# Seven row blocks of a hybrid decoder layer turned by transposing DMAs in place of TensorE, and the last value block of two FFN parts computed by feature

## The chip, the cores and the metric

The kernel runs on one core of a Trainium2 chip. The metric is the device time of one execution in microseconds (us), the median of several runs. TensorE (PE) multiplies, VectorE (DVE) and ScalarE (ACT) work beside it, GpSimd (POOL) here does little but issue DMAs that accumulate, and SyncE (SP) issues nearly all other DMAs.

## The reference

One decoder layer for 256 tokens of width 2048, all in float32. What matters here is its row of dense products:

```python
merged = (sigmoid(g_a) * (ret_out @ w_proj_ret) + sigmoid(g_b) * (rnn_out @ w_proj_rnn))
h = h + merged @ w_mix_out
hn = rmsnorm(h, norm_xa_w)
mem_n = rmsnorm(mem, norm_mem_w)
h = h + memory_cross_attention(hn, mem_n, xa_w_q, xa_w_k, xa_w_v, xa_w_o)
hn = rmsnorm(h, norm_ffn_w)
up = causal_dwconv(hn @ w_up, conv_w, conv_b)     # 2 x 5632 columns
gate, val = split(up, 2)
h = h + (silu(gate) * val) @ w_down
return rmsnorm(h, final_norm_w)
```

## The kernel before

**Precision and weights.** A float32 product is made of three products of parts: each operand is split into a high part `hi` and a rest `lo`, and hi·hi, hi·rest and rest·hi are summed. All weights lie in one array in the order of use and are streamed in pieces of 1 MB (`raw`, 128x2048, six buffers). `prefetch` keeps two pieces ahead: SP loads `raw` (L265), ACT casts `hi` (L286), DVE subtracts `lo` (L287), and PE reads both. There are three buffers of `hi` and of `lo`, so the cast of a piece waits until PE is through with the piece three before it. One piece is one *unit*; `later(n, fn)` lets `fn` be written into the program n+1 units on, and it is in this way that all other work is placed between the units.

**Products.** A product of 512 output columns is four units (four groups of four 128-row chunks of the 2048). `gemm_n` gives it by token (tokens on the partitions) into one accumulator: 16 matmuls with `hi` (L362, L363) and 8 with `lo` (L369) a unit. `gemm_t` gives it by feature (output columns on the partitions) into two accumulators: 16 matmuls of 512 and 16 of 256 columns a unit (L351). Accumulators come from a pool of three. Two neighbouring blocks of columns can be made as a pair (`pair_add`, `pair_out`) by seven products in place of eight: 11 units in the order q1 p0 q3 p1 q5 q2 q6 p2 q7 q4 p3, where a p unit has 24 matmuls and a q unit 12. For these, operands must exist as sums too: `ss` (four subtractions and additions on DVE, L501 to L504, then L506 and L507), and sums of weights are made in the `raw` buffers A, B and C: after q5's `lo`, DVE adds B to A (L294); when that is done, POOL issues a DMA that accumulates the weights of q7 onto B (L267); and a further addition on DVE (L292) makes the weights of q4. ACT casts the pieces in the order of the units, each `hi` behind the one before it on its queue.

**Turning.** A product contracts over features, so a row block (256 tokens by 512 columns) that came by token must be turned, each half of it (256 columns) giving one `s` (its hi and rest). Two ways exist. On PE: `transposed` makes four 128x128 transposes (L532) per half block into a buffer of PSUM, `sm`, of which there are two, and ACT and DVE read it (`split_pair`, L555 and L556; `split_cols` with the norm's weight, L578 and L579). By DMA: `row_planes` copies the block's words as two planes of 16 bits (ACT, L757, `rp`), `turn_planes` issues two transposing DMAs on SP (L1205, into `d`), and `join_planes` puts the words of each half together again (ACT, L763, two copies into `jp`). Of the row blocks before the FFN, twelve go by PE: the four of `merged` (`turn_merged`), the four of the residual stream after `w_mix_out` and the four after `xa_w_o` (`turn`, with `URGENT` priority for the scheduler). The blocks of the FFN's up product (`up`) go by DMA.

**The FFN** is cut into parts of 4, 4 and 3 blocks. In a part each block is a gate product and a value product, both turned by DMA, then the causal convolution (`conv`: ACT L1281, DVE L1283), then `hidden` (L1354 to L1356, and the split L555, L556), which gives two pairs of `hid`. After a part of four, two `pair_add` of `ffn_w_down` read all eight of `hid` (pairs 6 and 7 come of the part's last value block). They begin right behind the product of the last value block, whose joins are due 2 and 4 units on. In the part of three the last value block is already made by `gemm_t`, with `scaled` (ACT copies half the accumulator, L544; DVE adds the other half, L545, and scales, L676).

Of the kernel before, what the change touches and what calls it, by code (L numbers as in the profile page):

```python
# [12 lines left out]
U16 = mybir.dt.uint16  # L13
# [141 lines left out]
def hybrid_layer(  # L155
# [37 lines left out]
    def tmp(s="t"):  # L193
        return tp.tile([P, 2, S], F32, tag="tmp", name=nm(s))
# [109 lines left out]
    def later(n, fn):  # L304

        pending.append((step[0] + n + 1, fn))
# [460 lines left out]

    class KeptRows(list):
# [247 lines left out]
    def turn_merged(m, pr):  # L1016
        for t in transposed(m[:, :, pr * S : (pr + 1) * S]):
            if len(merged) < KC:
                c = tmp("mt")
                act.mul(c, t, 0.5)  # L1020
                merged.append(split_pair(c))
                merged_sums.append(sums(c))
            else:
                merged.append(split_pair(t, 0.5))
# [95 lines left out]
    rsms = []  # L1120
# [14 lines left out]
    h1s, h1s_sums = [], []  # L1135
    ss1 = residual("w_mix_out", merged, merged_sums, h1s, h1s_sums, p_xa, memory_steps)
    hkept = dp.tile([4, P, 2, BW], F32, name="hkept")
    for b in range(4):
        sp.dma_start(out=hkept[b], in_=hrow[b])

# [44 lines left out]
    def row_planes(o):  # L1185

        t = big([P, 2, 2, BW], U16, s="rp")
        planes(t, o)
        return t

# [9 lines left out]

    def turn_planes(rows):

        d = big([P, 2, KC, S], U16, s="d")
        for tt in range(2):
            sp.dma_start_transpose(  # L1205
                out=d.rearrange("p a c s -> p (a c) s")[:, :, tt * P : (tt + 1) * P],
                in_=rows[:, tt].rearrange("p a w -> p (a w)"),
            )
        return d
# [153 lines left out]
    for part, nb_ in enumerate(FF_PARTS):  # L1363
# [3 lines left out]
        for b in range(b0, b0 + nb_):  # L1367
# [10 lines left out]
            up(FF, b, None if last and not paired else (2, 4) if last else (1, 2), finish_up)  # L1378
# [54 lines left out]
```

## Time and profile before

| what | value |
|---|---|
| median of 3 runs | 1997.41 us (1996.22 to 1998.04) |
| the profiled execution | 1995.6 us, its span 1993.8 us |
| PE busy | 1968.6 us, 99% of the span |
| DVE, ACT, POOL busy | 79%, 64%, 2% |
| granted TensorE clock, mean | 0.995 |
| HBM | 220 GB/s over the span |

A row of a timeline reads: start, duration, engine, line, operation, output <- inputs, how many, and in brackets the idle time before it with what ended it. A row of a group reads: count, then busy us and mean ns of one, then the idle time before them. In a table of windows each engine has its busy time and, in brackets, its instructions; PEclk is the granted clock as a share of full speed. SPq and POOLq are the queues on which these engines issue.

### The profile page before, as it was taken

What the parts mean: (1) busy time and instruction counts of PE and PEld (TensorE: products, weight loads), DVE (VectorE), ACT (ScalarE), POOL (GpSimd) and SP (SyncE); (2) the same over time, 40 slices, a digit from 0 to 9 for tenths busy, and PEclk for the clock granted to TensorE, in tenths of its full rate; (3) what the DMA queues carried; (4) which work ended last, traced back from release to release, by engine and by line L of the source; (5) the groups of instructions that cost most, each with busy time, mean ns of one, the idle gap of its engine ahead of it and who ended that gap; (6) DMA issues with size and microseconds to landing.
All of it is one profiled execution on the core that took longest, in us unless ns stands there. A gap on an engine that the chain in (4) does not pass through costs nothing.

```text
span 1993.8 us, 23634 instructions
## 1 busy us (share of the span) xinstructions
PE 1968.6 (99%) x9304; PEld 1650.8 (83%) x9304; DVE 1566.4 (79%) x1546; ACT 1277.2 (64%) x1323; POOL 43.2 (2%) x52
## 2 busy tenths in 40 slices
PE   9999999999999999999999999999989999899998
PEld 7888888888888888888888888888878888788887
DVE  6978888889886886779988778677786777885775
ACT  6655656767677554567778756567744667546662
POOL 0000000000000000000000000000000000000000
PEclk9999999999999999999999999999999999899999
DMA  9675674655887865878998748766777677686671
GB/s 369 233 261 147 223 264 161 230 190 160 266 260 220 248 250 190 252 256 258 270 259 235 267 125 271 236 226 204 234 232 273 207 219 236 204 278 228 211 245 61
DMA packets 146463, 456.59 MB, mean 229 GB/s; under 512 B 77744, under 2 KB 82480, under 8 KB 98608
## 3 DMA queue, kind: packets, MB, share of 16 engines
q1 hardware_dynamic: 139072, 410.51, 58.7%
q0 software_dynamic: 5760, 41.95, 11.6%
q10 hardware_dynamic: 1520, 2.63, 0.4%
q8 instruction: 73, 1.20, 0.2%
q14 instruction: 38, 0.31, 0.0%
HBM read 420.96 MB, written 16.78 MB: 220 GB/s over the span
## 4 chain that ended last, share of the span: by engine, by line
PE 91%; DVE 4%; ACT 2%; DMA 1%; issue 1%; SPq 0%; POOLq 0%; ACTq 0%; DVEq 0%
PE acc L362 25%; PE acc L363 25%; PE acc L369 24%; PE acc L351 14%; PE sm L518 2%; DVE lo L287 1%; ACT hi L286 1%; DMA raw<-in_wall 1%; PE acc L518 1%; PE sm L948 1%; PE sm L532 1%; DVE raw L294 0%; DVE fv L1283 0%; DMA d<-rp 0%; DVE tb L722 0%
## 5 line engine op out<-in xcount | busy, mean ns | idle before, releaser
L287 DVE TENSOR_TENSOR lo<-raw,hi 128x2048 fp32r<-128x2048 f32 (+1 forms) x420 | 950.9, 2267 | 297.8 <-ACT hi L286 297.0
L286 ACT CAST hi<-raw 128x2048 fp32r<-128x2048 f32 (+1 forms) x418 | 793.2, 1901 | 522.7 <-PE acc L363 374.8
L362 PE MATMUL acc<-hi,s 128*128 128x512 f32 x2008 | 787.3, 392 | 12.4 <-ACT hi L286 12.3
L363 PE MATMUL acc<-hi,s 128*128 128x512 f32 x2008 | 784.3, 391 | 0.0
L369 PE MATMUL acc<-lo,s 128*128 128x512 f32 x2008 | 501.1, 389 | 0.0
L362 PEld LDWEIGHTS acc<-hi,s 128*128 128x128 f32 x2008 | 378.6, 189 | 91.5 <-ACT hi L286 13.2
L363 PEld LDWEIGHTS acc<-hi,s 128*128 128x128 f32 x2008 | 378.9, 189 | 78.5 <-DVE s L556 1.0
L369 PEld LDWEIGHTS acc<-lo,s 128*128 128x128 f32 x2008 | 377.1, 188 | 78.3
L351 PE MATMUL acc<-s,hi 128*128 128x512 f32 x832 | 200.4, 392 | 2.1 <-DVE hi L284 1.5
L351 PEld LDWEIGHTS acc<-s,hi 128*128 128x128 f32 x832 | 153.5, 188 | 32.8 <-issue 1.6
L362 PE MATMUL acc<-hi,ss 128*128 128x512 f32 x320 | 125.8, 393 | 0.8 <-ACT o L454 0.6
L363 PE MATMUL acc<-hi,ss 128*128 128x512 f32 x320 | 124.7, 390 | 0.0
L763 ACT COPY jp<-d 128x512 uint16<-128x512 uint16 x132 | 93.4, 771 | 29.4 <-DMA d<-rp 29.3
L351 PEld LDWEIGHTS acc<-s,lo 128*128 128x128 f32 x832 | 107.1, 191 | 4.9 <-DVE lo L287 1.3
L351 PE MATMUL acc<-s,lo 128*128 128x256 f32 x832 | 110.5, 284 | 0.5 <-DVE lo L287 0.5
L369 PE MATMUL acc<-lo,ss 128*128 128x512 f32 x320 | 85.6, 389 | 0.0
L362 PEld LDWEIGHTS acc<-hi,ss 128*128 128x128 f32 x320 | 60.1, 188 | 14.5 <-ACT o L454 1.4
L369 PEld LDWEIGHTS acc<-lo,ss 128*128 128x128 f32 x320 | 60.1, 188 | 12.6
L363 PEld LDWEIGHTS acc<-hi,ss 128*128 128x128 f32 x320 | 60.1, 188 | 12.2
L267 POOL DMA_DIRECT2D raw<-in_wall x40 | 35.2, 880 | 1550.7 <-DVE lo L287 887.5
L427 DVE TENSOR_TENSOR nat<-nat,acc 128x512 f32<-128x512 f32 (+1 forms) x49 | 44.0, 910 | 14.9 <-PE acc L369 14.9
L292 DVE TENSOR_TENSOR raw<-raw,raw 128x2048 f32<-128x2048 f32 x20 | 45.8, 2288 | 0.4
(235 smaller groups left out, 1251.7 us busy)
## 6 DMA issues: line engine op xcount, KB each, us to landing
raw<-in_wall SPq DMA_DIRECT2D x333, 1024.0 KB, 5.0
raw<-in_wall POOLq DMA_DIRECT2D x40, 1024.0 KB, 8.2
fkept<-nat SPq DMA_DIRECT2D x12, 512.0 KB, 7.7
nat<-fkept SPq DMA_DIRECT2D x12, 512.0 KB, 5.6
xt<-in_x_t SPq DMA_DIRECT2D x11, 256.0 KB, 7.8
raw<-in_wall SPq DMA_DIRECT2D x5, 512.0 KB, 7.9
nat<-in_x ACTq DMA_DIRECT2D x4, 512.0 KB, 10.1
ret<-hr SPq DMA_DIRECT2D x4, 512.0 KB, 4.6
```

The lines of the kernel that those rows point to most:

```text
L267: pool.dma_start(out=raw, in_=src, accum_op=ALU.add)
L286: act.copy(hi[:, a:b], raw[:, a:b])
L287: dve.tensor_tensor(out=lo[:, a:b], in0=raw[:, a:b], in1=hi[:, a:b].bitcast(F32), op=ALU.subtract)
L292: dve.tensor_tensor(out=to, in0=to, in1=by, op=ALU.add)
L351: pe.matmul(a, part, sx, start=k == 0 and t == 0, stop=k == nk - 1 and t == 0, skip_group_check=True)
L362: pe.matmul(o, h, hi, start=start and kk == 0, stop=False, skip_group_check=True)
L363: pe.matmul(o, l, hi, start=False, stop=False, skip_group_check=True)
L369: pe.matmul(o, h, lo, start=False, stop=stop and kk == KC - 1, skip_group_check=True)
L427: dve.tensor_tensor(out=o, in0=o, in1=i, op=op)
L518: ins = pe.matmul(o, a, b, start=start and i == 0, stop=stop and i == 2, skip_group_check=True)
L532: ins = pe.transpose(t[:, j, tt * P : (tt + 1) * P], rows[:, tt, k + j * P : k + (j + 1) * P], ident)
L763: ins = act.copy(words(t)[:, :, :, 1 - i], d[:, i, 2 * pr : 2 * pr + 2, :])
```

## The change

1. `merged` blocks 0, 1 and 2 are turned by `turn_merged_by_dma`, block 3 by PE as before. The joins are written 2 or 3 units on (1 or 2 for block 2). The factor 0.5 goes into `split_pair` and `sums`; the separate ACT multiplication falls away.
2. The residual's blocks 0 and 1, after `w_mix_out` and after `xa_w_o`, are turned by `turn_by_dma`, blocks 2 and 3 by PE as before. After `w_mix_out` the joins stand 1 and 2 units behind the transposing DMAs, after `xa_w_o` 3 and 4.
3. The stores of `h`'s blocks 0 and 1 to memory (`hkept`) are issued inside `turn_by_dma`; those of 2 and 3 stay behind `w_mix_out`.
4. The last value block of the two FFN parts of four is made by `gemm_t`, as the part of three has it; its convolution and `hidden` are due 1 and 3 units on.

```diff
+    def turn_merged_by_dma(m, n):
+        d = turn_planes(row_planes(m))
+
+        def join(pr):
+            t = join_planes(d, pr)
+            merged.append(split_pair(t, 0.5))
+            if len(merged) <= KC:
+                merged_sums.append(sums(t, 0.5))
+
+        for pr in range(2):
+            later(n + pr, lambda pr=pr: join(pr))
...
-        for pr in range(2):
-            later(pr, lambda m=m, pr=pr: turn_merged(m, pr))
+        if b < 3:
+            later(0, lambda m=m, n=2 if b < 2 else 1: turn_merged_by_dma(m, n))
+        else:
+            for pr in range(2):
+                later(pr, lambda m=m, pr=pr: turn_merged(m, pr))
...
-                for pr in range(2):
-                    later(i if bs[0] and len(bs) > 1 else 2 * i + pr, lambda b=b, pr=pr: turn(b, pr, out, osum, wcol))
+                if b < 2:
+                    n, m = ((0, 3), (4, 7))[i] if len(RESIDUAL[w]) == 2 else ((0, 1), (1, 2))[i]
+                    later(n, lambda b=b, m=m - n: turn_by_dma(b, m, out, osum, wcol))
+                else:
+                    for pr in range(2):
+                        later(i if len(bs) > 1 else pr, lambda b=b, pr=pr: turn(b, pr, out, osum, wcol))
...
+    def turn_by_dma(b, m, out, osum, wcol):
+        d = turn_planes(row_planes(hrow[b]))
+        if b < len(keep):
+            keep[b]()
+
+        def join(pr):
+            t = join_planes(d, pr)
+            i = 4 * b + 2 * pr
+            if osum is not None and len(out) < KC:
+                for j in range(2):
+                    act.activation(t[:, j, :], t[:, j, :], AF.Identity, scale=wcol(i + j))
+                out.append(split_pair(t))
+                osum.append(sums(t))
+            else:
+                out.append(split_cols(t, lambda j: wcol(i + j)))
+
+        for pr in range(2):
+            later(m + pr, lambda pr=pr: join(pr))
...
-            up(FF, b, None if last and not paired else (2, 4) if last else (1, 2), finish_up)
+            if last and paired:
+                for pr, a in enumerate(gemm_t("ffn_w_up", 0, h2s, NT, FF + b * BW)):
+                    later(1 + 2 * pr, lambda pr=pr, z=scaled(a, "uz"): finish_up(pr, z))
+            else:
+                up(FF, b, None if last else (1, 2), finish_up)
```

The order of instructions on each engine is set when the program is built, and the change moves it. Three places matter below; the numbers in the names tell buffers apart, and line numbers above 1000 differ between the two kernels.

**ACT at the end of the first `pair_add` of a part's down product.** Before, from the cast for p2 to that for q4: the casts are for p2, q7 and q4, `fv` is the convolution of pair 7, and `s_1672` is pair 7's split.

```order
L286 CAST hi_1674_11226<-raw_1673_11224 128x2048
L555 ACTIVATE s_1663_11157<-fo_1662_11153 128x2x256
L286 CAST hi_1676_11244<-raw_1652_11075 128x2048
L1281 ACTIVATE fv_1606_10757<-jp_1669_11206,pf_80 128x256 x2
L286 CAST hi_1678_11261<-raw_1640_10996 128x2048
L555 ACTIVATE s_1672_11221<-fo_1671_11217 128x2x256
```

And in the changed kernel, where `hi_1681`, `hi_1683` and `hi_1685` are the casts for p2, q7 and q4, and `s_1677` is pair 7's split:

```order
L555 ACTIVATE s_1669_11174<-fo_1668_11170 128x2x256
L286 CAST hi_1678_11239<-raw_1647_11015 128x2048
L286 CAST hi_1681_11257<-raw_1680_11255 128x2048
L286 CAST hi_1683_11275<-raw_1661_11114 128x2048
L555 ACTIVATE s_1677_11236<-fo_1676_11232 128x2x256
L286 CAST hi_1685_11292<-raw_1647_11015 128x2048
```

The convolution has left this place (it now stands ahead of q5's cast), and the split of pair 7, which stood behind the cast for q4, stands ahead of it; the cast for q7 is ahead of both. On PE, q4's first two matmuls stood behind p2's first four, the first of them ahead of all that read pair 7; now they stand behind all of p2.

**DVE at the start of the same `pair_add`.** Before, `lo_1646`, `lo_1654`, `lo_1657` and `lo_1659` belong to p0, q3, p1 and q5, the addition into `nat` takes q1's product, and `jp_1660` is the first joined half of the value block:

```order
L287 TENSOR_TENSOR lo_1646_11039<-raw_1644_11036,hi_1645_11038 128x2048
L287 TENSOR_TENSOR lo_1654_11078<-raw_1652_11075,hi_1653_11077 128x2048
L427 TENSOR_TENSOR nat_1634_10952<-nat_1634_10952,acc_1649_11072 128x512
L287 TENSOR_TENSOR lo_1657_11097<-raw_1655_11094,hi_1656_11096 128x2048
L287 TENSOR_TENSOR lo_1659_11126<-raw_1640_10996,hi_1658_11125 128x2048
L1271 TENSOR_TENSOR jp_1660_11142<-jp_1660_11142,rsb_379 128x512
```

Now, with the two accumulators of the value block (`acc_1636` and `acc_1637`) read there; `lo_1653`, `lo_1663` and `lo_1666` belong to p0, q3 and p1:

```order
L545 TENSOR_TENSOR uz_1655_11102<-acc_1636_10923,c_1654_11101 128x512
L676 TENSOR_TENSOR uz_1655_11102<-uz_1655_11102,rsb_379 128x512
L287 TENSOR_TENSOR lo_1663_11117<-raw_1661_11114,hi_1662_11116 128x2048
L545 TENSOR_TENSOR uz_1657_11107<-acc_1637_10924,c_1656_11106 128x512
L427 TENSOR_TENSOR nat_1641_10963<-nat_1641_10963,acc_1658_11111 128x512
L676 TENSOR_TENSOR uz_1657_11107<-uz_1657_11107,rsb_379 128x512
L287 TENSOR_TENSOR lo_1666_11136<-raw_1664_11133,hi_1665_11135 128x2048
```

The reading of the value block's second accumulator, `acc_1637`, now stands behind q3's rest. The pool of three gives that accumulator's place to p0's; before, p0's took the place of the value block's one accumulator, which ACT's copies into `rp` set free.

**DVE and PE at the start of the first `pair_out` of `xa_w_q`.** Before, DVE around the addition of `w_mix_out`'s block 3 to the residual (L1085); `s_1006` and `s_1011` are the two pairs of the residual's block 2:

```order
L579 SCALAR_TENSOR_TENSOR s_1006_6893<-sm_1005_6888,pb_79,s_1006_6893 128x256
L287 TENSOR_TENSOR lo_1014_6941<-raw_1012_6938,hi_1013_6940 128x2048
L579 SCALAR_TENSOR_TENSOR s_1006_6893<-sm_1005_6888,pb_79,s_1006_6893 128x256
L579 SCALAR_TENSOR_TENSOR s_1011_6933<-sm_1010_6928,pb_79,s_1011_6933 128x256 x2
L1117 TENSOR_REDUCE var_1018_6974<-ssm_6355 128x2
L612 TENSOR_SCALAR rv_1019_6976<-var_1018_6974 128x2
L450 TENSOR_SCALAR neg_1129_7657<-ro_1020_6978 128x2
L450 TENSOR_SCALAR neg_1174_7946<-ro_1020_6978 128x2
L287 TENSOR_TENSOR lo_1023_6983<-raw_1021_6980,hi_1022_6982 128x2048
L1085 TENSOR_TENSOR nat_942_6516<-nat_942_6516,acc_1001_6857 128x1024
L287 TENSOR_TENSOR lo_1036_7037<-raw_1034_7034,hi_1035_7036 128x2048
```

And now (the same addition is L1110, the pairs of block 2 are `s_1008` and `s_1013`, `sm_1006` and `ss_1005` are the sums of block 1's last pair, and `lo_1038` and `lo_1043` belong to q3 and p1):

```order
L502 TENSOR_TENSOR sm_1006_6882<-sm_1006_6882,jp_1003_6873 128x128
L1110 TENSOR_TENSOR nat_944_6515<-nat_944_6515,acc_999_6842 128x1024
L504 TENSOR_TENSOR sm_1006_6882<-jp_1003_6873,sm_1006_6882 128x128
L287 TENSOR_TENSOR lo_1038_7035<-raw_1036_7032,hi_1037_7034 128x2048
L507 TENSOR_TENSOR ss_1005_6881<-sm_1006_6882,ss_1005_6881 128x512
L579 SCALAR_TENSOR_TENSOR s_1008_6894<-sm_1007_6889,pb_79,s_1008_6894 128x256
L579 SCALAR_TENSOR_TENSOR s_1013_6934<-sm_1012_6929,pb_79,s_1013_6934 128x256
L287 TENSOR_TENSOR lo_1043_7064<-raw_1041_7061,hi_1042_7063 128x2048
L579 SCALAR_TENSOR_TENSOR s_1008_6894<-sm_1007_6889,pb_79,s_1008_6894 128x256
L579 SCALAR_TENSOR_TENSOR s_1013_6934<-sm_1012_6929,pb_79,s_1013_6934 128x256
```

The pairs of block 2, done before the addition until now, stand behind it and behind a sum of block 1. On PE, the first product (q1, `acc_1033`) ends and the second (p0, `acc_1035`) begins as follows; `acc_1034` is p1's accumulator, and `nat_944` is block 3 of the residual, turned into `sm_1039`:

```order
L369 MATMUL acc_1033_7029<-lo_1016_6942,s_1004_6878 128x512
L362 MATMUL acc_1035_7031<-hi_1024_6983,s_1008_6894 128x512
L362 MATMUL acc_1034_7030<-hi_1042_7063,s_1008_6894 128x512
L363 MATMUL acc_1035_7031<-hi_1024_6983,s_1008_6894 128x512
L363 MATMUL acc_1034_7030<-hi_1042_7063,s_1008_6894 128x512
L362 MATMUL acc_1035_7031<-hi_1024_6983,s_1008_6894 128x512
L362 MATMUL acc_1034_7030<-hi_1042_7063,s_1008_6894 128x512
L532 MATMUL sm_1039_7051<-cid_82,nat_944_6515 128x128 x4
L363 MATMUL acc_1035_7031<-hi_1024_6983,s_1008_6894 128x512
L362 MATMUL acc_1035_7031<-hi_1024_6983,s_1013_6934 128x512
```

Three of p1's matmuls now stand among p0's first, ahead of the transposes of block 3, which stood ahead of all p0's matmuls before.

More of the change, by code (lines that the diff above doesn't have):

```diff
@@ L766, in join_planes, with row_planes, turn_planes @@
         return t
+    def row_planes(o):
+        t = big([P, 2, 2, BW], U16, s="rp")
+        planes(t, o)
+        return t
+    def turn_planes(rows):
+        d = big([P, 2, KC, S], U16, s="d")
+        for tt in range(2):
+            sp.dma_start_transpose(
+                out=d.rearrange("p a c s -> p (a c) s")[:, :, tt * P : (tt + 1) * P],
+                in_=rows[:, tt].rearrange("p a w -> p (a w)"),
+            )
+        return d
     class KeptRows(list):
@@ L1017, in turn_merged @@
         for t in transposed(m[:, :, pr * S : (pr + 1) * S]):
[L1018 to L1024, printed above, removed]
+            merged.append(split_pair(t, 0.5))
[3 more added lines that the diff above has]
+            t = join_planes(d, pr)
+            merged.append(split_pair(t, 0.5))
+            if len(merged) <= KC:
+                merged_sums.append(sums(t, 0.5))
+        for pr in range(2):
+            later(n + pr, lambda pr=pr: join(pr))
     for b in range(4):
@@ L1118, in rstd_rows @@
         return rsqrt_small(var, 2, 1.0 / D, EPS)
-    rsms = []
+    rsms, keep = [], []
     ssm = sp_.tile([P, 2, 4], F32, tag="ss0", name="ssm")
@@ L1135, in hybrid_layer @@
     h1s, h1s_sums = [], []
+    hkept = dp.tile([4, P, 2, BW], F32, name="hkept")
+    keep += [lambda b=b: sp.dma_start(out=hkept[b], in_=hrow[b]) for b in range(2)]
     ss1 = residual("w_mix_out", merged, merged_sums, h1s, h1s_sums, p_xa, memory_steps)
-    hkept = dp.tile([4, P, 2, BW], F32, name="hkept")
-    for b in range(4):
+    for b in (2, 3):
         sp.dma_start(out=hkept[b], in_=hrow[b])
+    keep.clear()
     lscale = sp_.tile([P, 2], F32, tag="ls", name="lscale")
@@ L1183, in hybrid_layer @@
     qs = KeptRows("qs")
[L1185 to L1189, printed above, removed]
     for b in (0, 2):
@@ L1199, in hybrid_layer @@
             later(1 + 2 * i, lambda b=b + i, o=o: qs.store(b, row_planes(o)))
[L1201 to L1209, printed above, removed]
     def turn_key(b, o):
```

## The prediction

> **What bounds the kernel now.** First the busy table, the shares of the chain that ended last, and the one costly group that waits:
>
> ```profile
> PE 1968.6 (99%) x9304; PEld 1650.8 (83%) x9304; DVE 1566.4 (79%) x1546; ACT 1277.2 (64%) x1323; POOL 43.2 (2%) x52
> ...
> PE 91%; DVE 4%; ACT 2%; DMA 1%; issue 1%; SPq 0%; POOLq 0%; ACTq 0%; DVEq 0%
> ...
> L362 PE MATMUL acc<-hi,s 128*128 128x512 f32 x2008 | 787.3, 392 | 12.4 <-ACT hi L286 12.3
> ```
>
> PE is the bound: of the 1993.8 us span it idles 25.2. Time can go only where a PE instruction goes, where PE stops waiting, or where its clock stays up. Half of the idle time, 12.3 us, is one kind of wait: matmuls for ACT's cast of `hi`. The table of windows shows where (the first row is undisturbed):
>
> ```profile
> 1400.00:1450.00 50.00, 50.00 (x222) 41.43 (x221) 38.87 (x42) 36.51 (x38) 1.79 (x2) 1.00 0.74 214
> 1450.00:1500.00 50.00, 43.94 (x185) 35.56 (x184) 42.82 (x32) 23.75 (x18) 1.73 (x2) 0.93 0.75 238
> ...
> 1700.00:1750.00 50.00, 43.73 (x180) 35.24 (x179) 41.86 (x35) 27.14 (x24) 1.76 (x2) 0.90 0.66 197
> ```
>
> Both disturbed windows lie at the start of the down product of a part of four, and there the clock drops too (0.93, 0.90). PE's timeline in them, from p2's first matmul to q7's first:
>
> ```profile
> 1456.66 0.39 PE L362 MATMUL acc<-hi,s 128*128 128x512 f32 x1
> ...
> 1463.79 1.33 PE L362 MATMUL acc<-hi,s 128*128 128x512 f32 x2 [6.07 <-ACT hi L286]
> ...
> 1467.51 0.63 PE L362 MATMUL acc<-hi,s 128*128 128x512 f32 x1
> 1467.94 0.55 PE L363 MATMUL acc<-hi,s 128*128 128x512 f32 x1
> ...
> 1471.06 0.39 PE L362 MATMUL acc<-hi,ss 128*128 128x512 f32 x1
> ...
> 1720.85 0.39 PE L362 MATMUL acc<-hi,s 128*128 128x512 f32 x1
> ...
> 1728.19 1.33 PE L362 MATMUL acc<-hi,s 128*128 128x512 f32 x2 [6.28 <-ACT hi L286]
> ...
> 1736.35 0.40 PE L362 MATMUL acc<-hi,ss 128*128 128x512 f32 x1
> ```
>
> Between p2's first matmul and q7's stand 26 matmuls (24 of p2, two of q4). At the usual 0.227 us (a unit of 24 takes 5.44, below) they need 5.9 us; they took 14.4 and 15.5. So the places lose **8.5 and 9.6 us**, of which 6.07 and 6.28 are the wait and the rest slow matmuls behind it (1467.51 to 1467.94: 0.43 apart).
>
> Why the wait: p2 needs pair 7, whose split stands on ACT behind q4's cast, and so PE's order has q4's first matmul inside p2, ahead of pair 7. That cast is late. DVE, ACT and POOL in the first place:
>
> ```profile
> 1444.21 2.28 DVE L294 TENSOR_TENSOR raw<-raw,raw 128x2048 f32<-128x2048 f32 x1
> ...
> 1447.15 0.89 POOL L267 DMA_DIRECT2D raw<-in_wall  x1 [21.87 <-DVE fv L1283]
> ...
> 1455.34 1.92 ACT L286 CAST hi<-raw 128x2048 fp32r<-128x2048 f32 x1 [2.38 <-DMA raw<-in_wall]
> 1457.16 1.09 ACT L1281 ACTIVATE fv<-jp,pf 128x256 f32<-128x256 f32 x2
> 1461.84 1.90 ACT L286 CAST hi<-raw 128x2048 fp32r<-128x2048 f32 x1 [3.59 <-DVE raw L292]
> ...
> 1457.79 1.76 DVE L1283 SCALAR_TENSOR_TENSOR fv<-jp,pf,fv 128x255 f32<-128x255 f32 x4
> 1459.47 2.28 DVE L292 TENSOR_TENSOR raw<-raw,raw 128x2048 f32<-128x2048 f32 x1
> ```
>
> A chain: POOL issues q7's accumulating DMA 0.7 us after L294, it lands some 8 us later, q7's cast begins (1455.34), pair 7's convolution stands behind that cast on ACT, then on DVE, L292 behind the convolution, q4's cast behind L292 (1461.84), pair 7's split behind that. The convolution is there since its joins stand 2 and 4 units into the down product.
>
> **The change, part by part** (against the profiled execution, 1995.6 us).
>
> *Transposes off PE.* Starts of `lo` groups with four transposes between, and without:
>
> ```profile
> 750.69 1.98 PE L369 MATMUL acc<-lo,s 128*128 128x512 f32 x8
> 752.51 0.60 PE L532 MATMUL sm<-cid,o 128*128 128x128 f32 x4
> ...
> 756.62 1.98 PE L369 MATMUL acc<-lo,s 128*128 128x512 f32 x8
> ...
> 762.06 1.98 PE L369 MATMUL acc<-lo,s 128*128 128x512 f32 x8
> ```
>
> A unit takes 5.93 us with a group and 5.44 without: 0.49 a group. Seven blocks are 14 groups: **−6.8 us**. The Trainium skill (TensorE: Matmul & The Clock Gate, Part 4: PE-mode transpose) gives about 275 ns for one transpose in a kernel; the single duration here agrees (272 ns in the group's row), and by 56 of them one behind another it would be −15.4; the spacing of the units decides, since they overlap.
>
> *The last value blocks by feature.* One `gemm_t` product in the chain's list, seven units without a break:
>
> ```profile
> 344.81 38.94 PE acc L351 x224
> ```
>
> 224 matmuls are seven units of 32: 5.56 us a unit against 5.44, for eight units **+1.0 us**.
>
> *The two stalls.* The convolution no longer waits for DMAs: it stands ahead of q5's cast, pair 7's split comes right behind q7's, and PE has all of p2 ahead of q4. If nothing new is late, **−18.1 us**. What is late next, counted from T, the end of `gemm_t`:
>
> ```profile
> L287 DVE TENSOR_TENSOR lo<-raw,hi 128x2048 fp32r<-128x2048 f32 (+1 forms) x420 | 950.9, 2267 | 297.8 <-ACT hi L286 297.0
> L286 ACT CAST hi<-raw 128x2048 fp32r<-128x2048 f32 (+1 forms) x418 | 793.2, 1901 | 522.7 <-PE acc L363 374.8
> ...
> L545 DVE TENSOR_TENSOR uz<-acc,c 128x512 f32<-128x512 f32 x2 | 1.4, 682 | 0.0
> ...
> L556 DVE SCALAR_TENSOR_TENSOR s<-fo,s 128x512 fp32r<-128x512 f32 x22 | 15.0, 683 | 0.0
> ...
> raw<-in_wall POOLq DMA_DIRECT2D x40, 1024.0 KB, 8.2
> ```
>
> - p0's accumulator is the value block's second one; DVE reads it (L545) behind q3's `lo`, which is behind q3's cast, which begins when the last `hi` matmul of `gemm_t` frees a buffer, 8 short `lo` matmuls of (5.56 − 16 · 0.227)/16 = 0.12 before the end: T − 0.95 + 1.90 + 2.27 + 0.68 = T + 3.9. PE is there after q1, at T + 2.7: **1.2 us**. Behind p0 the whole queue of PE waits.
> - p0 then ends at T + 9.4, and q5's `lo`, `hidden`'s sum and L294 end near T + 15.0. POOL issues 0.7 later, the DMA lands at T + 23.9, q7's cast ends at T + 25.8. Pair 7's split (L556 0.68, ACT's half about as long) is behind it: T + 27.1. PE comes to pair 7 in p2 at 24.5 + 0.9 + 1.2 = T + 26.6: **0.5 us**. L292 then ends at T + 29.4, q4's cast at 31.3, and PE needs it at 31.6: nothing.
>
> Two places: +3.4 us. The ends: 0 (the casts come a little earlier) and, by the slowest landing of that DMA in the trace (11.8 us), 3.6 more at each place.
>
> *A new wait at xa_w_q.* Before, block 2 of the residual was turned ahead of the addition of block 3:
>
> ```profile
> L504 DVE TENSOR_TENSOR sm<-jp,sm 128x128 f32<-128x128 f32 x4 | 1.2, 292 | 0.1
> ...
> 890.30 0.48 DVE L579 SCALAR_TENSOR_TENSOR s<-sm,pb,s 128x256 fp32r<-128x256 f32 x1 [0.54 <-ACT s L578]
> ...
> 897.71 0.39 PE L362 MATMUL acc<-hi,s 128*128 128x512 f32 x1
> ...
> L506 ACT CAST ss<-sm 128x512 fp32r<-128x512 f32 x24 | 14.9, 620 | 12.1 <-DVE sm L504 12.1
> ...
> L578 ACT ACTIVATE s<-sm,pb 128x256 fp32r<-128x256 f32 x24 | 10.8, 470 | 7.5 <-DVE s L579 6.4 <-PE sm L532 1.1
> ...
> L1085 DVE TENSOR_TENSOR nat<-nat,acc 128x1024 f32<-128x1024 f32 x2 | 2.4, 1220 | 2.4 <-PE acc L369 2.3
> ```
>
> It was done (890.30) 6.9 us before `xa_w_q` began (897.71). Now (T' is the end of block 3's product) DVE does the addition first, 1.22, then a short sum, 0.29; ACT `ss` 0.62 and two L578, 0.94: T' + 3.1; then p1's cast: T' + 5.0. DVE: `lo` 2.27, `ss` (512 elements, as L545) 0.68, two L579 0.96, p1's `lo` 2.27, one more L579 0.48: T' + 8.2. Only then is an `sm` free for PE's transposes of block 3, which PE reaches, by its own pace, after q1 (2.7) and six matmuls (1.4), at T' + 4.1. **+4.1 us**, in pieces: about 2.2 for p1's cast, the rest further on. What is behind on PE is all of `xa_w_q`.
>
> *The rest, at nothing.* Seven blocks add to ACT 14 copies into `rp` and 28 into `jp`:
>
> ```profile
> L763 ACT COPY jp<-d 128x512 uint16<-128x512 uint16 x132 | 93.4, 771 | 29.4 <-DMA d<-rp 29.3
> ...
> L757 ACT COPY rp<-o 128x1024 uint16<-128x1024 uint16 x16 | 16.1, 1048 | 0.0
> ...
> d<-rp SPq DMA_TRANSPOSE x50, 3.4
> ```
>
> That is 14 · 1.05 + 28 · 0.77 = 36 us on an engine that idles 717. SP's queue takes 14 more transposing DMAs, 3.4 us to landing. The cover is casts two units ahead; without it a block costs up to a landing, 3.4 us, on PE: 0 to 24 us for seven. I take 0, by the nearest row: 132 copies waited 29.3 us in all, and PE idled 12.3 for `hi`, all at the two places above. In the two `pair_add` and the `pair_out` I count some 4 us between the casts and PE's need. The factor 0.5 and the moved stores: 0 to one DVE or ACT instruction, under 0.7.
>
> **Sum:** −6.8 + 1.0 − 18.1 + 3.4 + 4.1 = −16.4 us: 1979.2 for the profiled execution. The median of the runs stands 1.8 above that execution: **1981**.
>
> **The rivals.**
>
> 1. *No new wait shows* (orders on ACT and DVE resolve earlier than walked). For it: each of the three waits rests on sums of durations with 0.5 us of play. Against: the instructions do stand behind one another. 1981 − 7.5 = 1973.5. Chance 0.10.
> 2. *The new waits slow the clock too.* For it: both long waits had 2.4 and 3.3 us of slow matmuls behind them. At `xa_w_q` some 4 us of idle in 6 would add as much: 1984; with the down places as well, 1990. Against: no window but the two has a clock under 1. The Trainium skill (same page, Part 1: The HAM clock gate) says that the clock halves after an idle window of about 3.4 us that runs freely. By that rule 6 us must slow it, as the trace shows, 1.2 us must not, and the 4.1 us in pieces may or may not; no run here shows such a case yet. Chance 0.12.
> 3. *The change doesn't do what it says*: p2 stays bound by the accumulating DMA of 8.2 us, since pair 7's split is still behind a cast that waits for it, and stops as long. Then only the transposes go: 1997.4 − 6.8 + 1.0 + 4.1 = 1995.7, within the measurement. For it: the DMA waits for q5's `lo` and L294 as before, so its issue and landing hardly move. Against: from the landing to pair 7's split it was 6.5 us and q4's cast, 8.4; now it is q7's cast alone, 1.9. Chance 0.10.
> 4. *Slower*: the joins bring the old stall to other places. ACT works in order; a join that waits for `d` holds the next casts, and in a pair the cast of q5 starts L294, the accumulating DMA and q7. If the DMA into `d` lands over 4 us later than the cast can bear, PE stops as at the old places, 8.5 to 9.6 us each. Pairs with joins in or just ahead of them: one of `w_mix_out`, two of `xa_w_q`, two of `xa_w_o`. Two of these cancel the gain; three give 1981 + 27 = 2008. For it: the transposes queue on SP between the loads. Against: 132 joins now, and no such stall. Chance 0.18.
>
> **Chances.** Forecast 0.50, rivals 0.10, 0.12, 0.10, 0.18. This measurement can tell about 0.2%, 4 us, from no change. Faster by more: 0.50 + 0.10 + 0.12 = 0.72; within: 0.10; slower: 0.18. The range goes from 1972 (rival 1 with its play) to 1998 (rivals 2 and 3), and leaves out nearly all of rival 4; the forecast's own bounds, no new wait and two slowest landings, are 1973.5 and 1988.
>
> **What will show it.** Groups L532 at 40 matmuls in place of 96. The waits of 6 us gone, and both windows near x222 and clock 1.00. A wait of about 1.2 us at p0 of each down product, put down to L545, and about 0.5 in p2, for `s`. Near 900 us about 4 us of idle ahead of transposes of `nat`. Idle time of PE elsewhere unchanged. I am wrong if `hi` waits of several us appear within `w_mix_out`, `xa_w_q` or `xa_w_o`, if the clock falls below 1 near 900 us, or if q4 is still waited for.

## The result and the profile after

| | before | changed |
|---|---|---|
| median, us | 1996.81 (1995.15 to 2000.2, 10 runs) | 1992.57 (1988.98 to 1993.23, 10 runs) |
| ratio to before | | 0.9975, 95% interval 0.9965 to 0.9984 |
| the profiled execution, span | 1995.6, 1993.8 | 1993.04, 1991.2 |

The change gains 4.2 us (3 to 7 by the interval), where 16 were forecast. The time lies in the range of 1972 to 1998 and the direction is right, but three quarters of the gain are missing. That it lies in the range says little for the forecast, since the upper end was set for rivals 2 and 3.

The page of the changed kernel, the same rows as before:

```profile
PE 1968.6 (99%) x9312; PEld 1650.1 (83%) x9312; DVE 1567.7 (79%) x1550; ACT 1298.0 (65%) x1353; POOL 43.3 (2%) x52
...
PE 35%; DVE 4%; issue 3%; DMA 3%; ACT 2%; SPq 1%; POOLq 0%; ACTq 0%; DVEq 0%
...
L362 PE MATMUL acc<-hi,s 128*128 128x512 f32 x1944 | 760.3, 391 | 7.6 <-ACT s L555 4.5
...
L763 ACT COPY jp<-d 128x512 uint16<-128x512 uint16 x152 | 108.0, 771 | 45.3 <-DMA d<-rp 45.3
```

The 12.3 us of waits for `hi` are gone, and yet PE is busy for 1968.6 us as before, with 56 transposes fewer: busy time that a slower clock stretches hides a loss. (The chain of waits accounts for less than half the span here, so its shares aren't read.) The windows, the first two around the start of `xa_w_q` and the last two at the down products:

```profile
850.00:900.00 50.00, 47.93 (x210) 38.76 (x208) 30.28 (x36) 36.52 (x52) 0.89 (x1) 0.98 0.85 252
900.00:950.00 50.00, 47.56 (x200) 38.27 (x200) 44.98 (x51) 37.26 (x47) 3.19 (x4) 0.92 0.75 241
1450.00:1500.00 50.00, 49.03 (x215) 39.78 (x214) 46.44 (x33) 25.22 (x16) 2.63 (x3) 1.00 0.79 241
1700.00:1750.00 50.00, 47.87 (x208) 38.45 (x207) 47.57 (x40) 27.95 (x21) 1.76 (x2) 1.00 0.78 243
```

The windows of the down products have recovered (x215 and x208 in place of x185 and x180, clock 1.00). The two around 900 us now hold x210 and x200, with the clock at 0.98 and 0.92. Before, they were undisturbed:

```profile
850.00:900.00 50.00, 50.00 (x234) 41.34 (x233) 35.03 (x45) 32.97 (x52) 1.61 (x2) 1.00 0.77 260
900.00:950.00 50.00, 50.00 (x226) 41.41 (x225) 44.96 (x47) 38.29 (x41) 2.47 (x3) 1.00 0.82 255
```

There most of the gain went. PE's timeline of that place in the changed kernel:

```profile
894.92 0.39 PE L363 MATMUL acc<-hi,s 128*128 128x512 f32 x1
896.40 0.49 PE L362 MATMUL acc<-hi,s 128*128 128x512 f32 x1 [1.09 <-ACT s L552]
897.87 0.69 PE L363 MATMUL acc<-hi,s 128*128 128x512 f32 x1 [0.98 <-DVE s L553]
898.37 1.91 PE L369 MATMUL acc<-lo,s 128*128 128x512 f32 x4
900.84 0.79 PE L362 MATMUL acc<-hi,s 128*128 128x512 f32 x1 [0.57 <-ACT s L578]
903.00 0.79 PE L362 MATMUL acc<-hi,s 128*128 128x512 f32 x1 [1.36 <-ACT hi L286]
...
906.00 1.11 PE L532 MATMUL sm<-cid,nat 128*128 128x128 f32 x4 [0.51 <-DVE s L579]
...
907.34 0.63 PE L362 MATMUL acc<-hi,s 128*128 128x512 f32 x1
```

`xa_w_q` began at 893.78 (T'). The transposes of block 3 were foreseen at T' + 8.2 and came at T' + 12.2. The five waits are 4.5 us (the bracketed idle times); between them matmuls run slow (0.63 to 0.79 us), and in windows of 5 us the granted clock (the column behind POOL's) falls to half (it is half from 898.0 to 908.3):

```profile
895.00:900.00 5.00, 2.93 (x8) 1.58 (x6) 5.00 (x8) 3.33 (x5) 0.00 (x0) 0.80 0.66 165
900.00:905.00 5.00, 3.07 (x7) 1.77 (x6) 5.00 (x5) 4.17 (x7) 0.00 (x0) 0.50 0.84 328
905.00:910.00 5.00, 4.49 (x17) 3.40 (x16) 3.12 (x12) 3.40 (x10) 1.41 (x2) 0.68 0.64 229
```

The first two waits, for block 1's last pair (`s`, L552 and L553), were not foreseen at all.

Where each kernel's time went is read by marks that all of them have, starts on PE's timeline: the first matmul of the long by-feature products (272.49 before), the first `ss` product of `w_mix_out` (818.5), `xa_w_q` (906.7), `xa_w_o` (1180.2), the spreading of the norm (L605, 1271.6), the first `ss` product of the two paired down products (1440.3, 1704.5), the last part's `gemm_t` (1896.4), the last group of L518 (1968.1). The differences of neighbouring marks, one profile each, in us and good to about 0.1, before and then each kernel's difference from it (e1 to e11 are the experiments below):

| stretch | before | changed | e1 | e2 | e3 | e4 | e5 | e6 | e7 | e9 | e10 | e11 |
|---|---|---|---|---|---|---|---|---|---|---|---|---|
| 1 up to w_mix_out | 546.0 | −3.0 | −3.0 | −3.0 | 0.1 | −2.9 | −2.9 | −3.0 | −2.9 | −3.0 | 0.0 | −3.0 |
| 2 w_mix_out to xa_w_q | 88.2 | **8.4** | 0.2 | −0.9 | 0.0 | **9.9** | 2.1 | −1.6 | 0.2 | −0.9 | 0.0 | 0.4 |
| 3 xa_w_q, attention | 273.5 | 1.1 | 1.5 | 5.2 | 0.4 | 0.4 | 0.3 | 4.4 | 1.8 | 4.9 | 2.1 | −0.1 |
| 4 xa_w_o | 91.4 | −1.0 | −0.8 | −0.9 | 0.0 | −1.3 | −0.1 | −0.5 | −0.6 | −0.6 | 0.0 | 0.0 |
| 5 FFN to first down | 168.7 | 0.3 | 0.3 | 0.3 | 0.5 | −0.2 | 0.6 | 0.3 | 0.3 | 0.3 | 0.6 | 0.5 |
| 6 first to second down | 264.2 | −5.9 | −5.1 | −5.7 | −5.6 | −0.7 | −6.1 | −5.6 | −6.4 | −7.5 | −8.0 | −7.7 |
| 7 second down, last up | 191.9 | −6.4 | −8.2 | −6.2 | −8.3 | −0.6 | −8.3 | −6.6 | −9.5 | −7.7 | −9.6 | −9.6 |
| 8 last part | 71.7 | 3.3 | 1.4 | 1.4 | −0.2 | −0.2 | 1.2 | 1.4 | 1.4 | 1.7 | 0.0 | 1.5 |

For the changed kernel they sum to −3.2; with 0.6 at the start that is the −2.6 between the spans.

SP's queue says why block 1's pair was late, first as it was before:

```profile
859.44 6.65 SPq L265 DMA_DIRECT2D raw<-in_wall  x2
866.15 0.43 SPq L208 DMA_DIRECT2D nat<-in_mem  x1
```

and now:

```profile
856.05 5.46 SPq L778 DMA_TRANSPOSE d<-rp  x2
861.61 0.53 SPq L265 DMA_DIRECT2D raw<-in_wall  x1
862.24 5.38 SPq L778 DMA_TRANSPOSE d<-rp  x2
867.68 0.58 SPq L208 DMA_DIRECT2D nat<-in_mem  x1
```

Before, the third load of memory rows was issued 31.6 us ahead of `xa_w_q` (which began at 897.71), now 26.1 ahead: four transposing DMAs of 10.8 us stand in front of it. ACT squares those rows, and on ACT's timeline of the changed kernel the squares stand ahead of all joins of `w_mix_out`'s blocks:

```profile
872.44 0.63 ACT L1161 ACTIVATE junk<-nat 128x512 f32<-128x512 f32 x1 [6.53 <-DMA nat<-in_mem]
...
873.68 1.39 ACT L763 COPY jp<-d 128x512 uint16<-128x512 uint16 x2
```

ACT waited 6.53 us (2.52 before) with the joins behind it. Theory A: the stall comes of ACT's in-order wait for this load. Rivals: the order of DVE alone, as the forecast had it; the blocks left on PE; or the transposing DMAs landing late.

### The profile page after: what moved, and what is told of

Its sections match the earlier page's. It is cut to its first block, busy times and chain, and to the rows that moved or that the text cites. A ratio compares the mean times of both kernels' runs of the same rounds, so it can differ in the third digit from the quotient of the medians.

```text
span 1991.2 us, 23696 instructions
## 1 busy us (share of the span) xinstructions
PE 1968.6 (99%) x9312; PEld 1650.1 (83%) x9312; DVE 1567.7 (79%) x1550; ACT 1298.0 (65%) x1353; POOL 43.3 (2%) x52
## 5 line engine op out<-in xcount | busy, mean ns | idle before, releaser
L362 PE MATMUL acc<-hi,s 128*128 128x512 f32 x1944 | 760.3, 391 | 7.6 <-ACT s L555 4.5
L363 PE MATMUL acc<-hi,s 128*128 128x512 f32 x1944 | 759.1, 391 | 1.4 <-DVE s L553 1.0
L369 PE MATMUL acc<-lo,s 128*128 128x512 f32 x1944 | 486.0, 390 | 0.0
L362 PEld LDWEIGHTS acc<-hi,s 128*128 128x128 f32 x1944 | 366.2, 188 | 86.3 <-ACT s L555 5.7
L363 PEld LDWEIGHTS acc<-hi,s 128*128 128x128 f32 x1944 | 366.3, 188 | 77.6 <-DVE s L553 1.3
L369 PEld LDWEIGHTS acc<-lo,s 128*128 128x128 f32 x1944 | 365.4, 188 | 75.8
L351 PE MATMUL acc<-s,hi 128*128 128x512 f32 x960 | 232.5, 393 | 0.6 <-DVE hi L284 0.6
L351 PEld LDWEIGHTS acc<-s,hi 128*128 128x128 f32 x960 | 178.2, 189 | 36.4 <-issue 0.8
L763 ACT COPY jp<-d 128x512 uint16<-128x512 uint16 x152 | 108.0, 771 | 45.3 <-DMA d<-rp 45.3
L351 PEld LDWEIGHTS acc<-s,lo 128*128 128x128 f32 x960 | 124.3, 192 | 5.0 <-DVE lo L287 0.9
L351 PE MATMUL acc<-s,lo 128*128 128x256 f32 x960 | 127.5, 284 | 0.2 <-DVE lo L287 0.2
L362 PEld LDWEIGHTS acc<-hi,ss 128*128 128x128 f32 x320 | 60.1, 188 | 15.6 <-ACT o L454 1.4
L1305 DVE TENSOR_TENSOR jp<-jp,rsb 128x512 f32<-128x512 f32 x38 | 25.8, 688 | 27.0 <-ACT jp L763 26.8
```

What stands on the lines that cost most here:

```text
L351: pe.matmul(a, part, sx, start=k == 0 and t == 0, stop=k == nk - 1 and t == 0, skip_group_check=True)
L362: pe.matmul(o, h, hi, start=start and kk == 0, stop=False, skip_group_check=True)
L363: pe.matmul(o, l, hi, start=False, stop=False, skip_group_check=True)
L369: pe.matmul(o, h, lo, start=False, stop=stop and kk == KC - 1, skip_group_check=True)
L763: ins = act.copy(words(t)[:, :, :, 1 - i], d[:, i, 2 * pr : 2 * pr + 2, :])
L1305: dve.tensor_tensor(out=z, in0=z, in1=rsb2, op=ALU.mult)
```

## The experiments

**e1: w_mix_out's blocks 0 and 1 on PE again.** The stores of `hkept` then stand behind the product as before.

```diff
-                if b < 2:
+                if b < 2 and w != "w_mix_out":
...
```

> The changed kernel, but with blocks 0 and 1 of the residual after w_mix_out turned on PE again; merged, xa_w_o and the value blocks stay as changed. Theory A (the stall of about 10 us at the start of xa_w_q comes of these two blocks' way by DMA): four groups of transposes come back, +2.0 us, the stall goes, -10.3: 1992.6 - 8.3 = 1984, with no idle of PE between 890 and 910 us. Theory B (the stall belongs to blocks 2 and 3, whose turning on PE is scheduled the same in both): the stall stays and the time is 1994 to 1995.

Measured: 1981.82 us (1981.18 to 1984.41, 5 runs), ratio 0.9925 (0.991 to 0.994). Stretch 2 is back at 88.4 us (88.2 before). The windows of e1, to be held against the 0.98 and 0.92 above:

```profile
850.00:900.00 50.00, 50.00 (x235) 41.34 (x234) 34.97 (x48) 33.62 (x54) 2.30 (x3) 1.00 0.79 265
900.00:950.00 50.00, 50.00 (x224) 41.38 (x223) 45.86 (x44) 37.30 (x38) 1.77 (x2) 1.00 0.82 256
```

So the stall belongs to these two blocks: they were to bring 2.0 us and cost 8.4 in all. Theory B falls.

**e2: the third and fourth loads of memory rows three units earlier.**

```diff
-        squares(load_rows(mem, c), ssm, c)
+        squares(mrow[c] if c in mrow else load_rows(mem, c), ssm, c)
...
+                if c > 1:
+                    later(5 + 4 * c - (0, 0, 3, 3)[c], lambda c=c: mrow.update({c: load_rows(mem, c)}))
                 later(5 + 4 * c, lambda c=c: memory_rows(c))
```

> The changed kernel, but the third and fourth loads of memory rows are issued three units earlier, so that the third stands ahead of the four transposing DMAs of w_mix_out on SP's queue; their squares on ACT are due where they were. Theory A (ACT stood 6.5 us before the squares for that load, which stood behind 10.9 us of transposing DMAs on SP, and all joins were late behind it): the stall at xa_w_q shrinks from 10.3 to under 1, about 1982.5. Theory B (the order of DVE alone makes it, block 2's pairs behind the addition of block 3): 4 us of the 10 stay, about 1987. Theory C (the transposes into d themselves land late): no change, 1992 to 1993.

Measured: 1986.13 us (1981.57 to 1987.15, 5 runs), ratio 0.9938 (0.9922 to 0.9954). By the time this lies between A and B; the stretches decide: number 2 falls from 96.6 to 87.3 us, all of the stall, as A says, and stretch 3 takes 5.2 us that A didn't expect. Theory B isn't refuted by this, since the order on DVE changed too (see e6).

**e3: the value blocks alone**, on the kernel before (part 4 of the change, nothing else).

> The kernel before, with one part of the change alone: the last value block of the two FFN parts of four by feature. Theory A (the two stalls of 8.5 and 9.6 us go but for 1.7 and 2.7 us at pair 7): -18.1 + 4.4 + 1.0 = -12.7, so 1996.8 - 12.7 = 1984. Theory B (only part of that gain is real, since work behind it fills up, or the final part of the FFN loses 3 us whenever it begins earlier): 1987 to 1995.

Measured: 1982.93 us (1982.08 to 1983.2, 5 runs), ratio 0.9926 (0.991 to 0.9942). Theory A, within 1.1 us. This part alone gains 13 us, three times the whole change.

**e4: the seven blocks alone**, the last value blocks as before.

> The changed kernel with the last value blocks as before: only the seven row blocks turned by DMA. Theory A (as the two traces add up: -6.8 for transposes, +10.3 at xa_w_q, about +2 in the attention and xa_w_o): +5.5, so 2002. Theory B (the forecast's own sizes, -6.8 and +4.1): 1994.

Measured: 1999.81 us (1997.43 to 2000.81, 11 runs), ratio 1.0012 (1.0004 to 1.0021). Slower than before, by 2.4 us (by the ratio): the sign of A, with half its size (5.5), and not B's 1994. Its waits of PE show the old stalls beside the new one. Of the three waits in the first row two, 5.95 and 5.82 us, are the old stalls; the third, 1.36 us, and the other rows belong to the new one:

```profile
PE acc L362 <- ACT hi L286: 13.1, 3, 6.0
PE acc L362 <- ACT s L552: 1.9, 1, 1.9
PE acc L362 <- ACT s L578: 1.1, 1, 1.1
```

**e5: merged and the value blocks**, all residual blocks on PE (`if False` in place of e1's condition).

> The kernel before with two parts of the change: merged's blocks 0 to 2 by DMA, and the last value blocks by feature; all residual blocks turned on PE. Theory A (each part keeps its own size): e3_value_only 1982.9 less six groups of transposes, 2.9 us, 1980.0. Theory B (part of it is lost as in the whole change): 1982 to 1984. Beside e1_mix_by_pe (1981.8) it also prices the two blocks of xa_w_o by DMA: if this kernel is the faster, they cost more than their 2.0 us.

Measured: 1982.01 us (1979.95 to 1983.39, 5 runs), ratio 0.9922 (0.991 to 0.9935). Theory B: stretch 1 gains its 2.9, and stretch 2 loses 2.1, with a wait of 1.74 us for a cast in the pair of `w_mix_out` (at 833.7) that e1 doesn't show. Against e1 the two blocks of `xa_w_o` by DMA are worth nothing that can be measured.

**e6: the squares moved, and not their load.** The squares of the third memory rows are due three units later; their load stays on SP where the change has it.

```diff
...
-                later(5 + 4 * c, lambda c=c: memory_rows(c))
+                if c == 2:
+                    later(5 + 4 * c, lambda c=c: mrow.update({c: load_rows(mem, c)}))
+                later(5 + 4 * c + (0, 0, 3, 0)[c], lambda c=c: memory_rows(c))
```

> The changed kernel with one thing moved: the squares of the third memory rows are due three units later, so that on ACT they stand behind the joins of w_mix_out's blocks 0 and 1. Their load stands on SP where it was, behind the four transposing DMAs. Theory A (ACT, in order, waits 6.5 us for that load and everything behind is late): the stretch from the first ss product of w_mix_out to that of xa_w_q takes 87 to 88 us in place of 96.6, the time is 1983 to 1986. Theory B (the load's place on SP, or the transposes themselves, make the stall): no change, 1992.

Measured: 1984.9 us (1983.81 to 1989.29, 5 runs), ratio 0.9944 (0.9933 to 0.9956). SP's queue of e6 holds the load as late as before the mend, and ACT's joins don't wait for it; first SP's timeline:

```profile
854.89 5.92 SPq L778 DMA_TRANSPOSE d<-rp  x2
860.91 0.53 SPq L265 DMA_DIRECT2D raw<-in_wall  x1
861.55 5.35 SPq L778 DMA_TRANSPOSE d<-rp  x2
866.95 0.58 SPq L208 DMA_DIRECT2D nat<-in_mem  x1
```

and ACT's:

```profile
862.83 1.40 ACT L763 COPY jp<-d 128x512 uint16<-128x512 uint16 x2 [2.45 <-DMA d<-rp]
...
877.86 0.63 ACT L1161 ACTIVATE junk<-nat 128x512 f32<-128x512 f32 x1
```

The first join starts at 862.83 in place of 873.68 and stretch 2 takes 86.6 us in place of 96.6. Theory B falls: the load is as late as it was and the transposing DMAs are where they were, and yet the stall is gone. What moved is ACT's place for the squares. It isn't the only thing that moved: with the squares later, the program's order changes too, and block 2's pairs stand ahead of block 3's addition on DVE again (in e2 as well). ACT's wait and the order that the forecast saw went together, and no run takes one without the other. How much belongs to each can only be estimated, from the changed kernel and e4 (in the next section).

**e7: e1, with the second half of the value block due 2 units on in place of 3.**

```diff
-                    later(1 + 2 * pr, lambda pr=pr, z=scaled(a, "uz"): finish_up(pr, z))
+                    later(1 + pr, lambda pr=pr, z=scaled(a, "uz"): finish_up(pr, z))
```

> e1_mix_by_pe with the second half of the last value block's convolution due 2 units on in place of 3. By that pair 7's split stands on ACT ahead of q7's cast, which waits for the accumulating DMA. Theory A (what is left of the two old stalls, 0.6 to 2.1 us each, is pair 7's split behind that cast): both waits go, 1981.8 - 2.5 = 1979.3, and no wait of PE is put down to s L555 or L556 in the two products. Theory B (the convolution itself is too late on DVE): the waits and 1982 stay.

Measured: median 1980.29 us of 6 runs (five from 1978.86 to 1980.66 and one at 1996.73, which stays unexplained), ratio 0.9928 (0.9903 to 0.9953). Theory A: in e1 PE waited three times for `s` of L555, 3.8 us; here those waits are gone in the down products (two others, 0.32 and 0.41 us, are there in the first), and the one left lies in the last part. Stretches 6 and 7 are 2.6 us shorter than e1's; the intervals of the two ratios don't separate them. ACT's rows in the first down product show the order: pair 7's split, then q7's cast, which still waits for its DMA.

```profile
1453.32 0.64 ACT L555 ACTIVATE s<-fo 128x512 fp32r<-128x512 f32 x1 [1.62 <-DVE fo L1389]
1456.84 1.92 ACT L286 CAST hi<-raw 128x2048 fp32r<-128x2048 f32 x1 [2.88 <-DMA raw<-in_wall]
```

**e9: the whole change with both mends** (e6's and e7's).

> The changed kernel with both mends: the squares of the third memory rows three units later, and the second half of the last value block's convolution due 2 units on. Theory A (the two places are independent): e6_squares_late 1984.9 less the 2 us that e7_due_1_2 gained on e1_mix_by_pe, 1983. Theory B (what is gained at xa_w_q is spent again in the attention behind it whenever w_mix_out's blocks go by DMA): the stretch from the first ss product of xa_w_q to that of xa_w_o again takes 4 to 5 us more than before's 273.5.

Measured: median 1980.85 us of 6 runs (1977.45 to 1989.42), ratio 0.9918 (0.99 to 0.9936). By the time, theory A's 1983 holds within the scatter; but stretch 3 takes 4.9 us more than before, as theory B says. More than 4 us are seen there in the three kernels that have `w_mix_out`'s blocks by DMA and no stall in stretch 2 (e2, e6, e9: 5.2, 4.4, 4.9). PE's idle times tell where. In e6 and e9 there are two waits for `o` (L454, L470) in the first 25 us of the stretch, 1.9 and 1.8 us together, which no other kernel has there, and a wait ahead of L518 some 155 us into it, 1.5 and 1.6 us. This last one e10 has too, 1.57 us and a stretch longer by 2.1, with before's code up to the FFN, so it may be scatter. In e2 nearly all of the idle time is there (2.7 us, and the clock was half for 3.4 us behind it). What makes the two waits for `o` is open.

**e10: e3 with e7's due time**, and **e11: e10 with merged by DMA.**

> e3_value_only (the kernel before with the last value blocks by feature) with the second half due 2 units on in place of 3; no row block more by DMA. Theory A (pair 7's split ahead of q7's cast takes the waits of 1.3 and 0.4 us away, as it did in e7_due_1_2): 1982.9 - 2 = 1981. Theory B (the seven blocks by DMA are worth their 6.8 us less 0): it is 3 us or more slower than e7_due_1_2's 1980.3.

> e10_value_due_1_2 with merged's blocks 0 to 2 by DMA as well, all residual blocks on PE. Theory A (six groups of transposes less, nothing new late): 2.9 us under e10_value_due_1_2, about 1978. Theory B (the joins of merged cost w_mix_out a wait for a cast, as the 1.7 us that e5_merged_value showed there): about 1980, the same as e7_due_1_2.

Measured: e10 1980.5 us (1979.24 to 1981.31, 5 runs), ratio 0.9911 (0.9898 to 0.9923); e11 1979.0 us (1977.8 to 1983.01, 4 runs), ratio 0.9909 (0.9895 to 0.9922). Theory A for e10. For e11 the median lies between A and B and the interval is e10's: 0 to 3 us, not resolved. e11 is the fastest kernel here, 18 us under before; with none of the seven blocks by DMA e10 comes within its scatter.

## Why the prediction was wrong, step by step

The forecast for the profiled execution was 1979.2 us and it took 1993.04, so 13.8 us are missing. By the stretches, 6.3 are missing in stretch 2, 3.3 in the last part, 1.9 in stretches 6 and 7 and about 1 each in 3 and 4.

**Transposes off PE, −6.8.** The size was right where nothing else moved: six groups in stretch 1 gave 3.0 us, 0.49 a group. Stretch 4 gave 1.0 of its 2.0; most of the rest went to a wait of 0.73 us ahead of L605. Of `w_mix_out`'s 2.0, 1.5 were there when `xa_w_q` began (77.7 us from its mark to T', 79.2 before), and the stall took more.

**Value blocks by feature, +1.0.** 0.5 us a block in stretch 5 of e3: right.

**The two stalls, −18.1, and +3.4 that stays.** Right in kind; e3 measured −13.9 in stretches 6 and 7, one `gemm_t` (0.5) included, so −14.4 for the stalls, against −14.7. The changed kernel itself gained 12.3 there; 1.4 of the 1.6 us between it and e3 is one wait at the second place (2.02 us in place of 0.62). The chain came out by its times in the changed kernel (T is 1438.56): the accumulating DMA issued at T + 15.6 (forecast 15.7), q7's cast begun at T + 23.8 (23.9), pair 7's split done at T + 27.0 (27.1). (The view puts the cast's wait down to PE, but the accumulating DMA landed at 1462.29, 0.1 us before the cast began.)

```profile
1454.15 0.89 POOL L267 DMA_DIRECT2D raw<-in_wall  x1 [18.43 <-DVE s L556]
...
1462.39 1.91 ACT L286 CAST hi<-raw 128x2048 fp32r<-128x2048 f32 x1 [3.51 <-PE acc L363]
...
1464.86 0.69 DVE L556 SCALAR_TENSOR_TENSOR s<-fo,s 128x512 fp32r<-128x512 f32 x1 [1.37 <-ACT s L555]
```

One part of it was wrong. p0 doesn't wait for the value block's second accumulator:

```profile
1441.30 0.39 PE L362 MATMUL acc<-hi,s 128*128 128x512 f32 x1
...
1442.23 0.68 DVE L545 TENSOR_TENSOR uz<-acc,c 128x512 f32<-128x512 f32 x1
```

PE began p0 at T + 2.7, before DVE had read that accumulator, so p0's is in the place of the first one, and the sentence on the pool of three ahead of the prediction is wrong. The 1.2 us were not saved: PE came to pair 7 that much earlier and waited there, 0.98 us at the first place and 2.02 at the second (bracketed idle times). In six profiles with the due time of 3 (the changed kernel, e1, e2, e3, e5, e6) the first of the two idle times there lies between 0.2 and 1.9 us, and e7 shows that it ends with pair 7's place behind q7's cast.

**The new wait at xa_w_q, +4.1: the step that failed.** Stretch 2 grew by 8.4 us where −2.0 and +4.1 make 2.1. The forecast started its chain at T', with the addition of block 3, and took it that block 1 had been joined in time. It had put the transposing DMAs' stay on SP under "the rest, at nothing", with only the weights' casts as those who might wait. The load of the memory rows is also behind them, ACT's squares wait for that load, and the joins are behind the squares. So ACT was late by its wait of 6.53 us at 872, and the casts and joins that DVE needs were late with it: DVE came to the addition of block 3 at T' + 4.6 (898.34) and not at T'. From there on the forecast's chain held: 7.7 us to the transposes of block 3 (906.00), where it had 8.2.

```profile
898.34 1.22 DVE L1110 TENSOR_TENSOR nat<-nat,acc 128x1024 f32<-128x1024 f32 x1
```

e4, whose code is the same up to the FFN, repeats it with a longer wait (its T' is 894.43). ACT waited 0.83 us more, DVE came to the addition 0.83 us later behind T', the transposes came 0.82 us later, and from the addition to the transposes it was 7.7 us again:

```profile
873.91 0.63 ACT L1161 ACTIVATE junk<-nat 128x512 f32<-128x512 f32 x1 [7.36 <-DMA nat<-in_mem]
...
899.82 1.21 DVE L1110 TENSOR_TENSOR nat<-nat,acc 128x1024 f32<-128x1024 f32 x1
...
907.47 1.11 PE L532 MATMUL sm<-cid,nat 128*128 128x128 f32 x4 [0.51 <-DVE s L579]
```

An estimate by part, from these rows: the transposes came 8.1 us behind PE's own pace (T' + 12.2 against T' + 4.1). 4.1 of that is the forecast's own term, DVE's order (which no run has without the late start), and 4.0 is the late start, which the forecast had at nothing. Behind the transposes slow matmuls added some 1.1 us: from 906.00 to the first `ss` product at 912.71 it was 6.7 us, and by before's pace those 21 matmuls and two groups of transposes take 5.6. Together that is 9.2 us. Stretch 2 shows 8.4, since 1.5 had been gained before T' and three matmuls of p1 (0.7 us) moved into it from the next stretch. e1 takes the blocks away and the loss with them; e6 takes ACT's wait away, and with it the loss and the order.

Rival 2's mechanism came too, and with it one of the prediction's own signs of being wrong, a clock below 1 near 900 us. Rival 2 had priced it at 3 us. It cost less than the slow matmuls suggest: most of them stand ahead of the transposes, which came when DVE let them, and on ACT and DVE no wait between 898.34 and 906.00 is put down to PE. At full clock PE would have waited there instead. Only the 1.1 us behind the transposes are surely its cost.

**The last part, +3.3, in no step.** There PE waited 1.91 us for an `s`, with slow matmuls behind, in code that didn't change. On ACT's timelines, before and then changed, the joins of the last gate block came later against the cast ahead of them:

```profile
1900.22 1.91 ACT L286 CAST hi<-raw 128x2048 fp32r<-128x2048 f32 x1 [1.18 <-PE acc L351]
1906.74 2.04 ACT L763 COPY jp<-d 128x512 uint16<-128x512 uint16 x3 [4.61 <-DMA d<-rp]
```

```profile
1894.34 1.91 ACT L286 CAST hi<-raw 128x2048 fp32r<-128x2048 f32 x1 [0.58 <-PE acc L351]
1902.67 2.03 ACT L763 COPY jp<-d 128x512 uint16<-128x512 uint16 x3 [6.42 <-DMA d<-rp]
```

ACT waits 6.42 us for the transposing DMA in place of 4.61. The eight kernels with merged by DMA and the value blocks by feature lose 1.2 to 3.3 us there, e3, e4 and e10 nothing, so it isn't all scatter. PE's wait follows the landing of the second transposing DMA. Counted from the start of the last part's `gemm_t`, it lands at 11.38 us in e5, 11.72 in e1, 11.80 in e11 and 12.07 in the changed kernel, and PE waits 1.21, 1.55, 1.63 and 1.91 us; in before, e3, e4 and e10 it lands at 10.0 to 10.3 and PE waits at most 0.1. Why it lands later was not tried and stays open. The loss comes with both parts of the change and with neither alone: the spans of e3 and e4 differ from before's by −13.5 and +4.8, −8.7 together, where the whole change has −2.6, and most of what is missing lies here (3.7) and in stretch 7 (2.5).

**Rivals 1 and 3** fall (new waits were there; the stalls went). **Rival 4** placed the danger rightly, in ACT's order and the joins, but at another price (8.4 us in one stretch, no accumulating DMA in it), and for e4, the seven blocks alone, its sign came true.

## What to carry to other kernels

When DMAs are put into a queue, list every transfer behind them on that queue and ask for each who waits for it in order, not only for the stream that bounds the kernel: here a load of 512 KB for an unrelated statistic held ACT for 6.53 us, and the joins behind it came late. A part of a change that removes PE work (0.49 us a group) is worth having only if no engine in the new path stands in order behind a transfer; what was lost in that one stretch (8.4 us) is more than all fourteen groups were to save (6.8). And a change of several parts is priced by part: 13 us from the value blocks and less than nothing from the seven blocks were one number of 4, and not even their sum.

## What the runs showed of the hardware

**Two transposing DMAs issued right behind another DMA took SP about twice as long.** On SP's timelines of both kernels a pair of transposing DMAs takes 2.6 to 3.7 us when the issue of the last other DMA had ended 2.4 us or more before, and 5.0 to 6.2 us when that was under 2 us before (856.05 and 862.24 above); two pairs of before lie between, 3.8 and 4.4 us. What makes the difference wasn't tried. One pair of the changed kernel, where the issue ahead of it had ended 6.0 us before:

```profile
1354.64 2.62 SPq L778 DMA_TRANSPOSE d<-rp  x2
```

**Short idle times can halve PE's clock.** After 1.91 us of idle in the last part the next matmuls were 0.43 us apart, and the granted clock was half from 1928.83 to 1932.25. After 1.79 us in the second down product it stayed at 1.00:

```profile
1724.63 0.50 PE L362 MATMUL acc<-hi,s 128*128 128x512 f32 x1 [1.79 <-ACT s L555]
...
1928.44 0.91 PE L362 MATMUL acc<-hi,s 128*128 128x512 f32 x2 [1.91 <-ACT s L555]
...
1929.57 0.63 PE L362 MATMUL acc<-hi,s 128*128 128x512 f32 x1
1930.00 0.63 PE L363 MATMUL acc<-hi,s 128*128 128x512 f32 x1
```

What tells the two apart can be read from the records of the granted clock. In all twelve traces half clock begins a whole multiple of 3.41 us after the trace's first clock record, and, the end of the kernel left out, it lasts 3.41, 6.83 or 10.24 us. If the time is cut into such windows of 3.41 us, the 1.91 us of idle lie within one window, and the 1.79 us are split (the two windows hold 1.30 and 0.82 us of idle). Between the start and the end of the kernels, eight windows at full clock hold 1.91 to 3.41 us of idle, and half clock follows each of them; the most idle time without it is 1.80 us, in e2. The waits near 900 us are such a case: the first two, 2.07 us together, lie in the window that ends at 898.01.

The Trainium skill (TensorE: Matmul & The Clock Gate, Part 1: The HAM clock gate) asks for an idle window of about 3.4 us before the clock halves. The length agrees with the 3.41 us here, and the 6.07 and 6.28 us of before agree too. That PE be idle for all of it does not: 1.91 us within a window were enough, and the measurement decides.
